# A two-layer hybrid decoder step on one core: page table in one transfer, sums of squares by token, and the prompt's products moved from GpSimd to VectorE

## Chip, cores and metric

The kernel runs on one core of a Trainium2 chip. The metric is the device time of one execution in microseconds (us); three unprofiled runs of the kernel before gave 2775.24, 2779.84 and 2781.72 us, median 2779.84 us.

## The reference, cut to what matters

Two layers of a decoder trunk work on a prompt (16 meta tokens and 512 tokens) and on a sample group (8 sequences of 8 new tokens with 2048 cached positions each), 592 token columns in all. Every layer does

```
x += 0.5 * SwiGLU_1(rmsnorm(x))
h  = rmsnorm(x);  [z|xBC|dt|q|k|v] = h @ w_in
SSD group: causal conv, chunked state-space scan, gate, grouped rmsnorm
SB group:  q, k normed per head, stick-breaking attention, rmsnorm
x += concat(ssd, sb) @ w_out
x += 0.5 * SwiGLU_2(rmsnorm(x))

rms_norm(x)  = x / sqrt(mean(x*x) + 1e-6) * gain
sb attention: z = q.k/8 + bias;  log_stay = log_sigmoid(-z) (0 where masked)
              w = exp(log_sigmoid(z) + sum of log_stay over later keys);  o = w @ v
cached keys and values: cache[l][page_table], page_table is 8 x 16 int32
```

So each norm needs, for each token, the sum of squares over the model dimension; stick-breaking weights are a sigmoid times a running product of "stays" from the right; and the cached keys and values are found through the page table.

## The kernel before, in words

**Layout.** Activations lie feature-major: a tile holds 128 features (partitions) by 592 tokens (columns), eight tiles make the model dimension. A weight matrix is multiplied in units of 128 output features (`gemm`, L618). `raw` (L570) loads 512 KB of float32 weights into one of three buffers by a DMA that SyncE (SP) issues; `split` (L576) makes a rounded high part `whi` on ScalarE (L581) and a remainder `wlo` on VectorE (L582); `mm3` (L585) then issues three products for each of 8 feature tiles and each of two column halves of 296 tokens (L590): 48 products a unit, into two PSUM banks. After every product `step` (L595) advances the generators in `self.flows`, so small work is written in between the large products, one piece a product.

**Norms.** The large products run on values that are not yet divided by the norm; the factor R is applied when a unit is drained (`times_r`, L226). `factor` (L539) makes R in a flow, six times through `norm_end` (L565, two tiles of squares, `acc` and `sq`, L443 to L453) and twice in `mix_sb` (L1247, four tiles of squares). The flow is: some waiting steps; `sums` (L459): float32 products with a block of ones as the stationary operand and 512 and then 80 (or 64) columns of squares moving, for each tile of squares its own strip of output rows; `by_token` (L466): two ScalarE copies out of PSUM and five PE transposes, so that tokens lie on partitions; `gather_sums` (L484): small VectorE copies and additions; `rsqrt` (L504): some 14 VectorE instructions of 128x5; 20 waiting steps; `spread` (L518): ten products that spread the result over 128 rows; two ScalarE copies into R (L559). While the flow runs, `self.hold` keeps units from being drained. `queries` (L784) does the same for eight heads a token with four tiles of squares, one flow a tile, and then makes the scaled queries `qs` on which the sample's attention starts. `head_norm` (L851) and `normed` (L1195) use the same helpers.

**Page table.** `setup_rest` (L275), written in the program after the first of the three parts of the first feed-forward block, loads constants. L331 to L335 load the page table in 20 DMAs, already spread as the gathers want it: 16 into `ptk` (8 partitions by 8 entries each) and 4 into `ptv` (32 partitions by 32 entries), both constant tiles with a buffer of their own. L338 to L353 make the row numbers `ki` and `vi` of them on VectorE; the gathers of keys (L1462) and values (L1526) on GpSimd (POOL) read those. Other loads of `setup_rest` (L286, L294) go into the shared temporary buffers (`tmp`, tag "t", six of them).

**Prompt attention.** `pair_blocks` (L1288) runs 12 times a layer and does two heads each time: PE products z, two sigmoids on ScalarE (L1314, L1315), the running product `stay` on VectorE (L1273), and then the product of the two on POOL (L1318); in `rest` PE transposes it (L1325) and multiplies with the values. The same stretch has the sample's attention over the cached pages (`past`, L1433): gathers on POOL, 32x32 transposes on VectorE (L1468), and so on.

**Order.** The program is written once in a straight line; the framework's scheduler then orders each engine's instructions by a model of their times and by priorities, and an engine runs its queue strictly in that order. Within `mixer`, `ahead` (L605) gives work earlier priorities from the tables `PRI` and `UNIT` (L94 to L102), due times counted in instructions from the point `p0` (L711). Instructions whose operands are ready early in the model can be moved far ahead of where they are written, if their tile has a free buffer.

Of the kernel before, what the change touches and what calls it, by code (L numbers as in the profile page):

```python
# [11 lines left out]
I32 = mybir.dt.int32  # L12
AF = mybir.ActivationFunctionType
ALU = mybir.AluOpType
# [13 lines left out]
def const_arrays():  # L28
    p = np.arange(128)
    f = np.float32  # L30
    a32 = np.arange(32)
    c = {}
    c["ident"] = np.eye(128)
    c["ones"] = np.ones((128, 1))
    c["half"] = p[:, None] // 64 == np.arange(32)[None, :]
    o8 = np.zeros((128, 64))
    q64 = np.arange(64)
    same = q64[:, None] // 8 == q64[None, :] // 8
    o8[:64] = same
    c["one8"] = o8  # L40
    c["srep"] = p[:, None] % 32 == p[None, :] % 32
    a16 = np.arange(16)[None, :]
    c["sel16"] = (p[:, None] % 8 == a16 % 8) & (p[:, None] // 32 % 2 == a16 // 8)
    c["mko"] = ((p[:, None] // 8) % 4 == np.arange(4)[None, :])
    sm = np.zeros((128, 8))
    sm[:64] = q64[:, None] // 8 == np.arange(8)[None, :]
    c["seqm"] = sm
    dsel = np.zeros((128, 8))
    for h in range(8):
        dsel[h, h] = 1.0  # L50
        dsel[32 + h, h] = 1.0
    c["dsel"] = dsel
    c["koff"] = ((p % 8) * 16)[:, None]
    c["voff"] = ((p % 32) * 4)[:, None]
    c["kt16"] = np.broadcast_to(np.arange(16)[None, :], (128, 16))
    return {k: np.ascontiguousarray(v.reshape(128, -1)).astype(f) for k, v in c.items()}

# [47 lines left out]
class Kern:  # L105
# [169 lines left out]
    def setup_rest(self):  # L275
# [49 lines left out]
            nc.vector.tensor_copy(o[:, 0], v)  # L325
            nc.vector.tensor_scalar(o[:, 1], v, -1.0, None, ALU.mult)

        ptk = self.cst([128, 8], "ptk", I32)
        ptv = self.cst([128, 32], "ptv", I32)
        pt = I["page_table"]  # L330
        for g in range(16):  # L331
            nc.sync.dma_start(ptk[8 * g:8 * g + 8, :], pt[:, g].partition_broadcast(8))
        ptr = pt.rearrange("b (a x) -> x (b a)", x=4)
        for x in range(4):
            nc.sync.dma_start(ptv[32 * x:32 * x + 32, :], ptr[x].partition_broadcast(32))  # L335
        kf = self.cst([128, 8], "kf")
        vf = self.cst([128, 32], "vf")
        nc.vector.tensor_copy(kf, ptk)  # L338
        nc.vector.tensor_copy(vf, ptv)
        nc.vector.tensor_scalar(kf, kf, 128.0, self.c_koff, ALU.mult, ALU.add)  # L340
        nc.vector.tensor_scalar(vf, vf, 128.0, self.c_voff, ALU.mult, ALU.add)
        nc.vector.tensor_scalar(kf, kf, 0.5, None, ALU.mult)
# [116 lines left out]
    def sums(self, A, B, x, w, t, sel):  # L459

        n = self.c1 - self.c0 - 512
        for p, c, m in ((A, self.c0, 512), (B, self.c0 + 512, n)):
            self.nc.tensor.matmul(p[w * x:w * x + w, 0:m], sel, t[:, c:c + m], start=True, stop=True)  # L463
            yield

    def by_token(self, A, B, wait):  # L466

        nc = self.nc
        n = self.c1 - self.c0
        s = self.tmp("sums")  # L470
        nc.scalar.activation(s[:, 0:512], A, AF.Copy)
        nc.scalar.activation(s[:, 512:n], B[:, 0:n - 512], AF.Copy)
        for _ in range(wait):
            yield
        for i in range(4):
            nc.tensor.transpose(A[:, 128 * i:128 * i + 128], s[:, 128 * i:128 * i + 128], self.ident)
            yield
        nc.tensor.transpose(B, s[:, n - 128:n], self.ident)
        yield
# [4 lines left out]
    def gather_sums(self, A, B, n, w):  # L484

        nc = self.nc
        v = self.tok("rv", n=n)
        pA, pB = A.rearrange("p (g c) -> p g c", c=128), B.unsqueeze(1)
        for p, o in ((pA, v[:, 0:4]), (pB, v[:, 4:5])):
            if w:  # L490
# [13 lines left out]
    def rsqrt(self, v, n, inv):  # L504

        nc = self.nc
        y, w, hi, lo = self.tok("ry", n=n), self.tok("rw", n=n), self.tok("rhi", F32R, n), self.tok("rlo", F32R, n)
        nc.vector.tensor_scalar(v, v, inv, 1e-6, ALU.mult, ALU.add)
        nc.vector.tensor_scalar(y.bitcast(I32), v.bitcast(I32), -0.5, float(0x5f3759df), ALU.mult, ALU.add)
        for _ in range(3):  # L510
            nc.vector.tensor_tensor(w, y, y, ALU.mult)
# [27 lines left out]
    def factor(self, squares, inv, wait):  # L539
# [5 lines left out]
        def flow():  # L545
            for _ in range(wait[0]):
                yield
            A, B = self.own("po", [128, 512]), self.own("pw", [128, 128])
            w = 128 // len(squares)
            for x, s in enumerate(squares):  # L550
                yield from self.sums(A, B, x, w, s, self.c_ones.to_broadcast([128, w]))
            yield from self.by_token(A, B, wait[1])
            y, r = self.rsqrt(self.gather_sums(A, B, 1, w), 1, inv)
            nc.vector.tensor_copy(rt, y)
            for _ in range(wait[2]):
                yield
            yield from self.spread_all(r, 0, 1, A, B)
            for p, o in self.both(A, B, R):
                nc.scalar.activation(o, p, AF.Copy)  # L559
            self.hold = False  # L560
# [223 lines left out]
    def queries(self, win):  # L784
# [8 lines left out]
        def flow(m, s):  # L793
            for _ in range(wait[0]):
                yield
            yield from self.sums(A, B, m, 32, s, self.c_half)
            if m < 3:
                return
            yield from self.by_token(A, B[:, 0:128], wait[1])
            v = self.gather_sums(A, B[:, 0:128], 8, 0)  # L800
            rt2 = self.tok("rt2", n=1)
            nc.vector.tensor_tensor(rt2, self.rt, self.rt, ALU.mult)
            nc.vector.tensor_tensor(v, v, rt2.to_broadcast([128, 5, 8]), ALU.mult)
            y, r = self.rsqrt(v, 8, 1.0 / 64)
            self.r8, self.nr8 = (self.small(n, [128, 5, 8], bufs=1) for n in ("r8", "nr8"))
            for _ in range(wait[2]):
# [481 lines left out]
    def pair_blocks(self, q, k, OT, m, blocks, i):  # L1288
# [3 lines left out]
        o = 0  # L1292
# [14 lines left out]
        for hp in range(2):  # L1307
# [7 lines left out]
                nc.scalar.activation(s[:, s0:s0 + n], zv, AF.Sigmoid, scale=self.nr8[:, b, h:h + 1], bias=self.nb[:, c:c + 1])  # L1315
                self.stay(s, 128, s0, s0 + n)

            nc.gpsimd.tensor_tensor(e[:, 0:o - 1], e[:, 0:o - 1], s[:, 1:o], ALU.mult)  # L1318

        def rest():  # L1320
            wt = []
# [275 lines left out]
```

## Time and profile before

| | us |
|---|---|
| median of three runs | 2779.84 |
| the profiled execution | 2797.72 |
| its span (first to last instruction) | 2795.9 |
| PE (matmul) busy in it | 2656.9 |
| VectorE (DVE) busy | 1502.2 |
| ScalarE (ACT) busy | 994.7 |
| GpSimd (POOL) busy | 356.9 |
| mean granted PE clock, share of 2.4 GHz | 0.973 |

The profiled execution took 17.9 us longer than the median of the unprofiled runs. In the rows below, PE is the matmul array and PEld its weight loads; a matmul's duration holds its time through the pipeline, so products that follow each other 0.13 us apart are shown with 0.30 us each. A row of idle time names what ended the wait ("<-").

### The profile page before, as it was taken

The page shows a single profiled execution, that of the slowest core. Times are in us where ns is not written, and L with a number is a line of the kernel's source. Part 1 is how long each engine was busy: PE and PEld are TensorE (multiplying, and loading weights), DVE is VectorE, ACT ScalarE, POOL GpSimd, SP SyncE. Part 2 cuts the span into 40 slices and gives each one's busy share as a digit, 9 for nine tenths or more (in the row PEclk, how much of TensorE's full clock was granted, in tenths as well). Part 3 has the DMA queues.
Part 4 walks back from the last instruction along what each step waited for, and adds up shares of the span by engine and source line. Part 5 has one row for each costly group of instructions (what it writes and reads, how often), then busy time and mean ns, then how long its engine had stood idle before and what let it go on. Part 6 is the DMA issues. An engine that isn't in the chain of part 4 may idle for free.

```text
span 2795.9 us, 51271 instructions
## 1 busy us (share of the span) xinstructions
PE 2656.9 (95%) x21469; PEld 2472.6 (88%) x21469; DVE 1502.2 (54%) x2978; ACT 994.7 (36%) x1795; POOL 356.9 (13%) x336
## 2 busy tenths in 40 slices
PE   6999999999877999999999999999997789999999
PEld 5999999887655899999999999998885568999999
DVE  4444445386768564343554343454776776444444
ACT  2222224255645332222332222233565543322222
POOL 1000000023356010000000000000334541000000
PEclk8999999999979999999999999999998899999999
DMA  3232234347677222222222322244576772222222
GB/s 100 76 93 93 79 106 134 113 145 258 204 233 241 100 69 85 82 76 88 72 84 76 105 77 92 87 145 126 169 248 203 250 236 69 78 89 80 88 77 87
DMA packets 250279, 343.22 MB, mean 123 GB/s; under 512 B 38104, under 2 KB 201888, under 8 KB 250048
## 3 DMA queue, kind: packets, MB, share of 16 engines
q1 hardware_dynamic: 213184, 205.71, 23.8%
q0 software_dynamic: 36864, 134.23, 14.4%
q8 instruction: 168, 2.75, 0.4%
q14 instruction: 63, 0.52, 0.1%
HBM read 320.23 MB, written 19.66 MB: 122 GB/s over the span
## 4 chain that ended last, share of the span: by engine, by line
PE 59%; DVE 3%; ACT 2%; DMA 1%; issue 1%; POOL 0%; another core or an unknown queue 0%; SPq 0%; DVEq 0%; ACTq 0%; POOLq 0%
PE g L590 52%; PE v L905 1%; DMA v<-in_cache_v,vi 1%; DVE kt L1468 1%; PE po L206 1%; PE po L463 0%; PE po L209 0%; PE sc L209 0%; DMA kn<-in_cache_k,ki 0%; PE z L209 0%; POOL v L1526 0%; PE z L206 0%; ACT L1090 0%; ACT dec L1090 0%; DVE x L777 0%
## 5 line engine op out<-in xcount | busy, mean ns | idle before, releaser
L590 PE MATMUL g<-xh,wlo 128*128 128x296 f32 (+1 forms) x3392 | 1014.6, 300 | 17.3 <-DVE wlo L582 17.3
L590 PE MATMUL g<-xl,whi 128*128 128x296 f32 (+1 forms) x3392 | 1015.9, 300 | 2.7 <-DVE xl L441 2.7
L590 PE MATMUL g<-xh,whi 128*128 128x296 f32 (+1 forms) x3392 | 1014.7, 300 | 2.4 <-DVE gs L229 2.0
L581 ACT ACTIVATE whi<-raw 128x512 fp32r<-128x512 f32 (+1 forms) x664 | 413.9, 624 | 1342.5 <-PE g L590 1271.1
L582 DVE TENSOR_TENSOR wlo<-raw,whi 128x512 fp32r<-128x512 f32 (+1 forms) x664 | 450.9, 679 | 614.5 <-ACT whi L581 568.4
L590 PEld LDWEIGHTS g<-xh,wlo 128*128 128x128 f32 x3392 | 640.4, 189 | 20.6 <-DVE wlo L582 17.9
L590 PEld LDWEIGHTS g<-xh,whi 128*128 128x128 f32 x3392 | 640.0, 189 | 10.5 <-issue 6.3
L590 PEld LDWEIGHTS g<-xl,whi 128*128 128x128 f32 x3392 | 640.5, 189 | 7.5 <-DVE xl L441 3.6
L590 PE MATMUL g<-hl,whi 128*128 128x296 f32 (+1 forms) x1408 | 417.9, 297 | 0.0
L590 PE MATMUL g<-hh,wlo 128*128 128x296 f32 (+1 forms) x1408 | 417.7, 298 | 0.0
L590 PE MATMUL g<-hh,whi 128*128 128x296 f32 (+1 forms) x1408 | 416.8, 298 | 0.0
L1462 POOL DMA_INDIRECT kn<-in_cache_k,ki x128 | 134.7, 1052 | 1590.6 <-PE g L590 1104.8
L590 PEld LDWEIGHTS g<-hl,whi 128*128 128x128 f32 x1408 | 265.2, 188 | 0.0
L590 PEld LDWEIGHTS g<-hh,wlo 128*128 128x128 f32 x1408 | 264.3, 188 | 0.0
L590 PEld LDWEIGHTS g<-hh,whi 128*128 128x128 f32 x1408 | 263.9, 188 | 0.0
L1468 DVE STREAM_TRANSPOSE kt<-kn 128x512 f32<-128x512 f32 x256 | 162.9, 681 | 29.0 <-PE pS L1097 7.5
L1526 POOL DMA_INDIRECT v<-in_cache_v,vi x128 | 139.1, 1087 | 252.3 <-DVE kt L1468 121.3
L686 DVE SCALAR_TENSOR_TENSOR x<-g,x 128x296 f32<-128x296 f32 (+1 forms) x192 | 88.2, 464 | 120.5 <-PE g L590 119.9
L229 DVE TENSOR_TENSOR us<-g,R 128x296 f32<-128x296 f32 (+1 forms) x176 | 81.5, 464 | 128.0 <-PE g L590 127.9
L229 DVE TENSOR_TENSOR gs<-g,R 128x296 f32<-128x296 f32 (+1 forms) x176 | 80.7, 464 | 125.9 <-PE g L590 120.0
L673 ACT ACTIVATE hh<-us 128x592 fp32r<-128x592 f32 (+1 forms) x88 | 61.4, 698 | 63.3 <-DVE us L671 63.3
L209 PE MATMUL sc<-kt,qbd 128*32 128x128 f32 x1920 | 79.0, 291 | 3.7 <-issue 3.6
(387 smaller groups left out, 2993.2 us busy)
## 6 DMA issues: line engine op xcount, KB each, us to landing
raw<-in_ffn_w_gu SPq DMA_DIRECT2D x176, 512.0 KB
raw<-in_ffn_w_down SPq DMA_DIRECT2D x80, 512.0 KB
raw<-in_w_in SPq DMA_DIRECT2D x44, 512.0 KB
raw<-in_w_out SPq DMA_DIRECT2D x16, 512.0 KB
spill<-x SPq DMA_DIRECT2D x16, 296.0 KB
x<-spill SPq DMA_DIRECT2D x16, 296.0 KB
raw<-in_ffn_w_down SPq DMA_DIRECT2D x16, 256.0 KB
xt<-in_x_prompt SPq DMA_DIRECT2D x8, 256.0 KB
```

What stands on the lines that cost most here:

```text
L206: i = self.nc.tensor.matmul(*a, **k).ins
L209: i = self.nc.tensor.matmul(*a, **k).ins
L229: self.nc.vector.tensor_tensor(tv[0:P, h, :], ps[h][0:P, 0:self.n], rv[0:P, h, :], ALU.mult)
L581: nc.scalar.activation(hi[:, 0:nk], s, AF.Copy)
L582: nc.vector.tensor_tensor(lo[:, 0:nk], s, hi[:, 0:nk].bitcast(F32), ALU.subtract)
L590: nc.tensor.matmul(ps[h][:, 0:self.n], w[:, k, :], self.hv(x)[:, h, :], start=(first and k == 0 and i == 0), stop=(last and k == nk - 1 an ...
L673: nc.scalar.activation(hh[:, a:b], u[:, a:b], AF.Copy)
L686: nc.vector.scalar_tensor_tensor(v, p, 0.5, v, ALU.mult, ALU.add)
L905: nc.tensor.matmul(ps[c], x[:, t0:t0 + 128], w.rearrange("p x c -> p (x c)"), start=(k == 0 and i == 0), stop=(k == 7 and i == 2))
L1462: nc.gpsimd.indirect_dma_start(kn, None, self.kflat, bass.IndirectOffsetOnAxis(ap=self.kidx[l][:, s, i:i + 1], axis=0))
L1468: nc.vector.transpose(kt[:, 2 * u:2 * u + 2].rearrange("p t h i -> p t (h i)"), kns[u][:, :, 256 * quad:256 * quad + 256])
L1526: nc.gpsimd.indirect_dma_start(v.rearrange("p k c -> p (k c)"), None, self.vflat, bass.IndirectOffsetOnAxis(ap=self.vidx[l][:, i, e:e + 1] ...
```

## The change

Five things are changed and nothing else. (1) The page table is loaded by one DMA into all 128 partitions (a temporary tile), made float32, and the entries that a partition needs are picked by a product with a 0/1 mask (two new constants, `mg` and `mx`) and halving additions on VectorE. (2) `factor` uses the new `token_sums`: for each group of 128 tokens and each tile of squares one float32 product with the squares as the stationary operand and one column of ones moving, so that the sums come out with tokens on partitions; the copies, transposes and gathering additions of that norm are gone. (3) `queries` does the same with two columns for its two heads a tile. (4) Two helpers get tiles of their own (`rg`, `rv`, `rq`). (5) The product of L1318 goes from GpSimd to VectorE.

```diff
@@ const_arrays
+    c["mg"] = p[:, None] // 8 == a16
+    c["mx"] = p[:, None] // 32 == np.arange(4)[None, :]
@@ setup_rest
-        ptk = self.cst([128, 8], "ptk", I32)
-        ptv = self.cst([128, 32], "ptv", I32)
-        pt = I["page_table"]
-        for g in range(16):
-            nc.sync.dma_start(ptk[8 * g:8 * g + 8, :], pt[:, g].partition_broadcast(8))
-        ptr = pt.rearrange("b (a x) -> x (b a)", x=4)
-        for x in range(4):
-            nc.sync.dma_start(ptv[32 * x:32 * x + 32, :], ptr[x].partition_broadcast(32))
+        pti = self.tmp("pti", [128, 128], I32)
+        nc.sync.dma_start(pti, I["page_table"].rearrange("b g -> (b g)").partition_broadcast(128))
+        ptf, sel = self.tmp("ptf", [128, 128]), self.tmp("sel", [128, 128])
+        nc.vector.tensor_copy(ptf, pti)
         kf = self.cst([128, 8], "kf")
         vf = self.cst([128, 32], "vf")
-        nc.vector.tensor_copy(kf, ptk)
-        nc.vector.tensor_copy(vf, ptv)
+        for out, m in ((kf, self.c_mg), (vf, self.c_mx)):
+            n, k = out.shape[1], m.shape[1]
+            sv = sel.rearrange("p (a g) -> p a g", g=k)
+            nc.vector.tensor_tensor(sv, ptf.rearrange("p (a g) -> p a g", g=k),
+                                    m.unsqueeze(1).to_broadcast([128, n, k]), ALU.mult)
+            while k > 1:
+                k //= 2
+                d = out.unsqueeze(2) if k == 1 else sv[:, :, 0:k]
+                nc.vector.tensor_tensor(d, sv[:, :, 0:k], sv[:, :, k:2 * k], ALU.add)
@@ Kern
+    def token_sums(self, out, squares, sel):
+        for i, t0 in enumerate(self.groups()):
+            for x, t in enumerate(squares):
+                self.nc.tensor.matmul(out[:, i], t[:, t0:t0 + 128], sel, start=(x == 0), stop=(x == len(squares) - 1))
+                yield
@@ gather_sums
-        v = self.tok("rv", n=n)
+        v = self.tok("rg", n=n)
@@ rsqrt
-        nc.vector.tensor_scalar(v, v, inv, 1e-6, ALU.mult, ALU.add)
+        s, v = v, self.tok("rv", n=n)
+        nc.vector.tensor_scalar(v, s, inv, 1e-6, ALU.mult, ALU.add)
@@ factor
-            w = 128 // len(squares)
-            for x, s in enumerate(squares):
-                yield from self.sums(A, B, x, w, s, self.c_ones.to_broadcast([128, w]))
-            yield from self.by_token(A, B, wait[1])
-            y, r = self.rsqrt(self.gather_sums(A, B, 1, w), 1, inv)
+            P = B[:, 0:5].unsqueeze(2)
+            yield from self.token_sums(P, squares, self.c_ones)
+            y, r = self.rsqrt(P, 1, inv)
@@ queries
-            yield from self.sums(A, B, m, 32, s, self.c_half)
+            P = A[:, 0:40].rearrange("p (g h) -> p g h", g=5)
+            yield from self.token_sums(P[:, :, 2 * m:2 * m + 2], [s], self.c_half[:, 0:2])
             if m < 3:
                 return
-            yield from self.by_token(A, B[:, 0:128], wait[1])
-            v = self.gather_sums(A, B[:, 0:128], 8, 0)
-            rt2 = self.tok("rt2", n=1)
+            rt2, v = self.tok("rt2", n=1), self.tok("rq")
...
-            nc.vector.tensor_tensor(v, v, rt2.to_broadcast([128, 5, 8]), ALU.mult)
+            nc.vector.tensor_tensor(v, P, rt2.to_broadcast([128, 5, 8]), ALU.mult)
@@ pair_blocks
-            nc.gpsimd.tensor_tensor(e[:, 0:o - 1], e[:, 0:o - 1], s[:, 1:o], ALU.mult)
+            nc.vector.tensor_tensor(e[:, 0:o - 1], e[:, 0:o - 1], s[:, 1:o], ALU.mult)
```

## Rows read from the trace of the kernel before

**Rows 1.** The page: span, and busy time of each engine.
```profile
span 2795.9 us, 51271 instructions
PE 2656.9 (95%) x21469; PEld 2472.6 (88%) x21469; DVE 1502.2 (54%) x2978; ACT 994.7 (36%) x1795; POOL 356.9 (13%) x336
```

**Rows 2.** Windows: stretch and length, busy us of each engine, PEclk, DMA share, GB/s.
```profile
0.00:100.00 100.00, 72.51 (x442) 66.17 (x443) 47.32 (x109) 29.87 (x54) 13.54 (x21) 0.88 0.34 91
...
740.00:900.00 160.00, 121.23 (x1355) 81.82 (x1352) 117.94 (x241) 83.77 (x176) 89.36 (x84) 0.83 0.68 221
...
2120.00:2260.00 140.00, 111.43 (x1207) 76.31 (x1206) 107.25 (x217) 80.42 (x166) 77.23 (x72) 0.83 0.67 218
```

**Rows 3.** Windows of L590 alone: length, PE and PEld busy (count), PEclk, DMA.
```profile
100.00:120.00 20.00, 20.00 (x150) 20.00 (x149) 1.00 0.26 80
40.00:72.00 32.00, 9.77 (x42) 9.24 (x43) 0.63 0.23 52
...
481.70:494.80 13.10, 10.58 (x72) 9.61 (x70) 1.00 0.45 141
```

**Rows 4.** Timeline of VectorE, ScalarE, PE in the start-up: start, length, operation [idle before].
```profile
55.51 0.18 DVE L339 CAST vf<-ptv 128x32 f32<-128x32 int32 x1 [20.50 <-DMA ptv<-in_page_table]
...
55.88 0.68 DVE L582 TENSOR_TENSOR wlo<-raw,whi 128x512 fp32r<-128x512 f32 x1
...
55.79 0.35 ACT L989 ACTIVATE dtw<-dtr 128x32 fp32r<-128x32 f32 x2 [19.61 <-DMA dtr<-in_w_in]
...
56.62 0.61 PE L590 MATMUL g<-xh,wlo 128*128 128x296 f32 x1 [16.64 <-DVE wlo L582]
```

**Rows 5.** Timeline of SyncE's DMA queue in the start-up: start, time to issue.
```profile
15.19 5.48 SPq L332 DMA_DIRECT2D ptk<-in_page_table  x9
...
24.95 2.48 SPq L332 DMA_DIRECT2D ptk<-in_page_table  x7
...
32.50 12.40 SPq L335 DMA_DIRECT2D ptv<-in_page_table  x4
44.94 3.19 SPq L984 DMA_DIRECT2D dtr<-in_w_in  x1
```

**Rows 6.** Line 286: shortest/median/longest issue in ns, first and last start.
```profile
L286 SPq DMA_DIRECT2D mt<-in_c_mask x2: 374/412/450, 156.9 to 157.4; - x2
```

**Rows 7.** Groups of VectorE by form: busy, mean ns; the nearest to the new operations.
```profile
L242 DVE CAST identr<-call 128x128 fp32r<-128x128 f32 x1 | 0.2, 227 | 1.9 <-DMA call<-in_c_const 1.9
...
L964 DVE TENSOR_TENSOR xc<-cacc,u 128x528 f32<-128x528 f32 x12 | 8.5, 711 | 2.9 <-ACT u L962 1.9 <-issue 1.0
```

**Rows 8.** Timeline of PE: sums of a norm between large products; four small products (L1543).
```profile
483.04 1.07 PE L463 MATMUL po<-sq,call 128*64 128x512 f32 x2
484.04 0.41 PE L590 MATMUL g<-xh,whi 128*128 128x296 f32 x1
...
650.96 0.62 PE L1543 MATMUL po<-call,ob 128*128 128x16 f32 x4
```

**Rows 9.** Timeline of PE in the second layer's output norm.
```profile
2328.69 1.07 PE L463 MATMUL po<-gsq,call 128*32 128x512 f32 x6
...
2340.01 0.33 PE L206 MATMUL po<-identr,rhi 128*128 128x128 f32 x1 [2.21 <-DVE rhi L514]
```

**Rows 10.** Groups of POOL by form: busy, mean ns, idle before.
```profile
L1318 POOL TENSOR_TENSOR be<-be,st 128x511 f32<-128x511 f32 x32 | 35.7, 1117 | 20.4 <-DVE st L1273 17.3 <-DVE te L1064 1.9 <-issue 0.8
...
L1318 POOL TENSOR_TENSOR be<-be,st 128x255 f32<-128x255 f32 x16 | 15.0, 947 | 18.7 <-DVE st L1273 15.4 <-DVE rv L498 3.1
```

**Rows 11.** Line 1505 on VectorE: ns shortest/median/longest; its group: busy, mean.
```profile
L1505 DVE SCALAR_TENSOR_TENSOR pbe<-pbe,cq,pst x32: 711/741/2202, 616.6 to 2295.0; 128x511 f32<-128x511 f32 x32
...
L1505 DVE SCALAR_TENSOR_TENSOR pbe<-pbe,cq,pst 128x511 f32<-128x511 f32 x32 | 28.7, 898 | 0.2
```

**Rows 12.** Waits of PE: us in total, times, longest.
```profile
PE po L206 <- DMA v<-in_cache_v,vi: 16.3, 9, 7.5
...
PE zt L1325 <- POOL be L1318: 6.0, 5, 3.1
```

## The prediction, made before the change was run

> **What bounds the kernel now.** I read the page first: PE is busy 2656.9 of 2795.9 us [rows 1], so at most 139 us of the span are PE's idle time, and what shortens the kernel is either such idle time or PE work. The windows then show where it is idle: 27.5 us in the first 100 us, 38.8 us in the first layer's mixing stretch (740 to 900) and 28.6 us in the second's (2120 to 2260), where the granted clock is 0.83 too [rows 2]. In the feed-forward blocks PE has no gap: 150 large products in 20 us, one every 0.133 us [rows 3].
>
> The timeline of the start-up shows the one large wait of the program. VectorE stood 20.50 us at the cast of `ptv`; the `wlo` behind it in its queue came only then, and PE waited 16.64 us for that [rows 4]. On SyncE's queue the 20 page-table DMAs took 5.48, 2.48 and 12.40 us to issue, 20.4 us in all [rows 5]. ScalarE stood beside it, 19.61 us for `dtr` [rows 4], which SyncE could issue only after them [rows 5].
>
> **The change part by part.**
>
> *The page table.* Twenty DMAs go, one of 128 rows of 512 bytes comes. Its target is now a temporary tile of tag "t". The other constants that load into that tag were not pulled ahead into the start-up: `mt` was issued at 156.9 us [rows 6], when the first feed-forward part no longer wants these buffers. I expect the new transfer and all that hangs on it (`ptf`, `kf`, `vf`, `ki`, `vi`, and on POOL's queue the first gathers of keys) there too; the sample's scores need them only in the mixer, after the whole block. The new VectorE work is one cast, two products and six additions of at most 128 columns: 9 by 0.23, the nearest row, a cast of 128x128 [rows 7], 2.1 us, between feed-forward products where PE's own time covers it; if it were at the start-up instead, 2 us is what it costs.
>
> What goes: between 40 and 72 us PE did 42 large products [rows 3], which at 0.133 are 5.6 us; with ten spreading products and five transposes at 0.12 (below), 1.8 us, that is 7.4 us of work in 32. So 24.6 us were lost, of them 16.64 the wait itself. The rest, 8.0 us, is half clock (0.63 mean in that window [rows 3]) and the wait for R. Without the gap the clock should hold, and R's chain of small VectorE instructions runs beside the next unit; but three units of 48 products fill the six PSUM banks, so a part of the wait for R stays. I take 16.6 and two thirds of 8.0: **-22**. Bounds: -24.6 if all goes, -10 if another late load takes over (first rival).
>
> *Sums by token, PE's work.* A norm of two tiles now: in the 13.1 us from 481.7 PE did 72 large products, 9.6 us, so sums and transposes cost 3.5 us. After: ten products, each two passes (as the eight instructions of today's four sums show). Four small ones with a 128-column stationary operand took 0.62 us, about 0.12 from start to start [rows 8]: 20 by 0.12 is 2.4. Each time a float32 product stands between the large ones there is more: the large product behind one shows 0.41 instead of 0.30 [rows 3, 8]; I take 0.2 an excursion for both edges, and five excursions (the half on `acc` is ready early, that on `sq` goes in one run): 3.4. So -0.1 a norm, six norms, -0.6. The output norm loses: today its sums run side by side in strips, six passes in 1.07 us [rows 9], in all about 3.3 with the transposes; after, 40 by 0.12 is 4.8: +1.5, twice, +3. Queries: four tiles at about 1.4 each [rows 8] and 0.6 of transposes, 6.2; after, 40 by 0.12 and four excursions, 5.6: twice -0.6. Sum about **+1**.
>
> *Sums by token, the wait for R.* Two ScalarE copies, the transposes and six small VectorE instructions leave the chain to R. Where PE had run out of banks this shows: the second layer's output norm waited 2.21 us for `rhi` [rows 9], and the waits at the start-up are counted above. I take -2.2 there and about -1 for the other places: **-3**. In the flow the steps of a norm go from 47 to 48, so that in a unit of 48 products the release of `hold` slips behind the unit's end and its drain is written one unit later; the scheduler orders by readiness and three units fit the banks, so I cost it at nothing. If it binds it is some 1 us at each of six norms. Norms together **-2**, bounds -6 and +8.
>
> A rule of the Trainium skill says otherwise of PE's work. The row first: two passes of 512 columns took 1.07 us, 0.5 apart [rows 8]. The page "TensorE: Matmul & The Clock Gate", section "Back-to-back issue gap", prices a product at its columns over 2.4 GHz plus 2.5 ns (0.216 us for 512), and its section "LDWEIGHTS (loading the stationary operand)" a load at columns over 1.2 GHz (0.107 us for 128). By it today's norm would be 4 by 0.216, 4 by 0.036 and 5 by 0.107, 1.5 us, and the new one 20 by 0.107, 2.1 us: the change would lose 0.6 a norm, six times, and the total would be 4 us less of a gain. The trace's 3.5 us does not agree with it, so I keep the rows.
>
> *The products on VectorE.* POOL spent 35.7 and 15.0 us on 32 and 16 of them [rows 10]. On VectorE a product of 528 columns of float32 took 0.711 [rows 7], so 0.69 for 511 and at most 0.41 for 255: 22 + 6.6 = 28.6 us over both layers. Against it: L1505 has a median of 0.741 but a longest of 2.202 us [rows 11], and its slow ones fall on times when POOL runs such a product; its mean is 0.898, so 32 by 0.157, 5 us, come back, and the scans suffer in the same way. Net about +23 in stretches where VectorE is busy 118 of 160 and 107 of 140 us [rows 2], so three quarters of the time; I put a quarter of it on the path: +6. Queued behind each new instruction are the transposes and splits of the same stretch. On the other side POOL no longer stands waiting for scans (17.3 + 15.4 us [rows 10]) ahead of its gathers, and PE waited 6.0 us for these products and 16.3 for gathered values [rows 12]: I take all of the first and a fifth of the second, -9. Sum **-3**. Bounds: -15 with both waits gone and no cost, +23 with all of it on the path.
>
> **The sum**: -22 - 2 - 3 = -27 us, against the profiled execution's 2797.7 (span 2795.9 and 1.8 around it): 2770.7. The runs shown have a median 17.9 us lower; I take the same 27 us off it: 2779.8 - 27 = **2753**.
>
> **Rivals.**
> 1. *Another late load takes the stall's place.* ScalarE waited for `dtr` nearly as long as VectorE for the table [rows 4]. It landed within 10.9 us of its issue at 44.94 [rows 4, 5]. Issued at 32.5 and as slow, it would hold ScalarE to 43 us, and PE would still stop for some 4; or the new table is pulled ahead and VectorE waits for it. Against: `dtr` was slow because 4-byte transfers were ahead of it. The start-up then gives -12, the whole -17: **2763**.
> 2. *VectorE becomes the bound of the mixing stretches (slower).* It decides once VectorE is busy more than about 95% there: 118 + 14 of 160 is 83%, which speaks against; that VectorE's queue is strictly in order speaks for, since a late scan then holds the transposes behind it. Then the whole 28.6 is on the path, and with a clock of 0.83 [rows 2] that falls further in longer PE gaps I add half: +43, with -25 from the rest +18: slower, **2797**.
> 3. *The new order gives back what the start-up gains.* Priorities inside the mixer are counted in instructions and the scheduler models times; other times there mean another order of the whole stretch, in which PE idles 67 us today [rows 2]. A loss of 40% of that, 27, is no change: **2780**.
>
> **How the numbers follow.** Forecast 0.70, rival 1 0.14, rival 2 0.08, rival 3 0.08. About 0.2%, 5.6 us, is what a measurement of this kernel can tell from no change. Faster: 0.70 + 0.14 and a quarter of rival 3's spread, 0.86; same 0.05 and slower 0.09 from the rest of it and rival 2. The likeliest case by its own bounds (the start-up 2 better to 5 worse, norms 4 better to 5 worse, products 10 better to 8 worse, not all at once) is 2740 to 2765. The range reaches past rival 1 above and a little below: 2735 to 2773.
>
> **What would show it.** Right: no wait of VectorE for a page-table transfer; PE's idle time in the first 100 us below 13 us instead of 27.5; the 42 products after the 40th us done by about 50; no L1318 on POOL, 48 more products on VectorE at 0.6 to 0.7 us, L1505 without values near 2 us; no wait for `rhi` in the second output norm; PE's extra at a norm still about 3.4. Wrong: a gap of over 5 us at the start-up behind ScalarE's `dtw` or the new cast; VectorE over 95% busy between 740 and 900; PE idle there above 50 us.

## The result and the profile after

The changed kernel took 2739.24 us (median of four runs, 2729.76 to 2747.8) against 2779.51 of the kernel before beside it: ratio 0.986, 95% interval 0.9833 to 0.9887, 40.3 us less. The forecast was 2753 (27 less), range 2735 to 2773. The profiled execution took 2746.03 us, its span is 51.9 shorter than the one of [rows 1]; 11 of that is the spread between executions, since before's profiled execution lay 17.9 above its median and this one 6.8.

The page of the changed kernel, and its windows at the times of [rows 2] (what stands in a window is some 20 us further on in the program than before):

```profile
span 2744.0 us, 51377 instructions
PE 2641.0 (96%) x21587; PEld 2497.2 (91%) x21587; DVE 1502.8 (55%) x2993; ACT 976.7 (36%) x1769; POOL 313.4 (11%) x288
```
```profile
0.00:100.00 100.00, 90.18 (x595) 85.72 (x596) 53.53 (x109) 34.92 (x61) 12.44 (x20) 0.97 0.34 102
740.00:900.00 160.00, 138.00 (x1521) 106.15 (x1519) 115.07 (x256) 76.61 (x165) 59.70 (x56) 0.89 0.67 229
2120.00:2260.00 140.00, 118.43 (x1328) 89.55 (x1328) 99.93 (x230) 67.00 (x145) 53.17 (x48) 0.91 0.67 227
```

PE is idle 9.8 us in the first 100 instead of 27.5, and 22.0 instead of 38.8 from 740 to 900; the granted clock is higher in all three. VectorE, which got 48 products more, is not busier over the span (1502.8 us against 1502.2).

To see where the 51.9 us come from I took marks on PE's timeline, each the start of a named large product, and subtracted:

| from, to | before | after | difference |
|---|---|---|---|
| start to the first product of the first down projection (`g<-hh`) | 154.3 | 134.3 | -20.0 |
| end of a first feed-forward block to the last value product, both layers | 63.3, 63.4 | 60.5, 60.5 | -5.7 |
| mixing stretch: last value product to the last product of the first half of `w_out` (`g<-mh`), both layers | 441.4, 435.8 | 426.4, 423.7 | -27.1 |
| all else | 1637.6 | 1638.6 | about +1 |

The two stretches as windows (columns as in [rows 2]), before, then the changed kernel:

```profile
544.90:986.30 441.40, 387.82 (x3945) 313.39 (x3944) 311.06 (x684) 220.30 (x451) 159.53 (x147) 0.93 0.60 196
1924.80:2360.60 435.80, 385.61 (x3945) 312.08 (x3944) 310.91 (x685) 222.92 (x453) 161.02 (x148) 0.93 0.60 199
```
```profile
522.20:948.60 426.40, 382.41 (x3963) 320.32 (x3962) 311.52 (x700) 215.45 (x444) 136.93 (x123) 0.92 0.60 203
1884.40:2308.10 423.70, 382.74 (x3964) 318.62 (x3963) 308.98 (x700) 214.07 (x442) 137.48 (x123) 0.93 0.60 204
```

PE's idle time in them falls from 53.6 and 50.2 us to 44.0 and 41.0, at nearly the same granted clock. The two mixing stretches carry half of the 51.9, and in the prediction's sum they have only -3. That is what the experiments are about.

**The start-up** is as forecast. L602 (before: L590) in the windows of [rows 3], then the longest gap between large products that is left there, and the page table with what used to wait for it (SyncE, VectorE):

```profile
40.00:50.00 10.00, 7.88 (x46) 7.49 (x45) 0.84 0.17 54
...
40.00:72.00 32.00, 29.88 (x202) 29.49 (x201) 0.93 0.16 52
```
```profile
15.14 0.38 SPq L995 DMA_DIRECT2D dtr<-in_w_in  x1
...
31.51 0.37 SPq L995 DMA_DIRECT2D dtr<-in_w_in  x1
...
47.80 0.41 PE L602 MATMUL g<-xh,whi 128*128 128x296 f32 x1 [1.22 <-DVE gs L231]
...
139.55 0.51 SPq L332 DMA_DIRECT2D pti<-in_page_table  x1
...
143.80 0.23 DVE L334 CAST ptf<-pti 128x128 f32<-128x128 int32 x1 [1.14 <-DMA pti<-in_page_table]
```

In the 32 us where PE had done 42 large products it now does 202. The wait of 16.64 us [rows 4] is gone, and no gap between large products in the first 100 us is longer than the 1.22 us behind `gs`. The new transfer goes out at 139.55, late, as `mt` did [rows 6], and VectorE waits 1.14 us for it under feed-forward products. The two transfers of `dtr`, of which the first left SyncE at 44.94 [rows 5] and the second at 57.77, leave at 15.14 and 31.51.

**The products and their neighbours**, groups of VectorE by form (line, form, count, busy and mean, idle before):

```profile
L1329 DVE TENSOR_TENSOR be<-be,st 128x511 f32<-128x511 f32 x32 | 21.1, 664 | 0.0
...
L1516 DVE SCALAR_TENSOR_TENSOR pbe<-pbe,cq,pst 128x511 f32<-128x511 f32 x32 | 23.7, 739 | 0.2
...
L1284 DVE TENSOR_TENSOR_SCAN st<-st,zero 128x255 f32<-128x255 f32 x16 | 10.7, 675 | 2.6 <-ACT st L1326 2.6
...
L1329 DVE TENSOR_TENSOR be<-be,st 128x255 f32<-128x255 f32 x16 | 6.4, 408 | 0.1
```
```profile
L1273 DVE TENSOR_TENSOR_SCAN st<-st,zero 128x255 f32<-128x255 f32 x16 | 14.3, 899 | 5.4 <-ACT st L1315 5.4
```

The last line is the kernel before's. The products cost 21.1 + 6.4 = 27.5 us. L1516 (L1505 in [rows 11]) fell from 28.7 to 23.7, the scan of 255 columns from 14.3 to 10.7: with no GpSimd product beside them these two groups give back 8.6 of the 27.5 us.

### The profile page after: what moved, and what is told of

It is laid out like the page before. It is cut to its first block, busy times and chain, and to the rows that moved or that the text cites. A ratio compares the mean times of both kernels' runs of the same rounds, so it can differ in the third digit from the quotient of the medians.

```text
span 2744.0 us, 51377 instructions
## 1 busy us (share of the span) xinstructions
PE 2641.0 (96%) x21587; PEld 2497.2 (91%) x21587; DVE 1502.8 (55%) x2993; ACT 976.7 (36%) x1769; POOL 313.4 (11%) x288
## 3 DMA queue, kind: packets, MB, share of 16 engines
q1 hardware_dynamic: 208016, 205.77, 23.7%
## 5 line engine op out<-in xcount | busy, mean ns | idle before, releaser
L602 PE MATMUL g<-xl,whi 128*128 128x296 f32 (+1 forms) x3392 | 1018.7, 301 | 0.9 <-DVE xl L447 0.9
L602 PE MATMUL g<-xh,wlo 128*128 128x296 f32 (+1 forms) x3392 | 1013.5, 300 | 3.4 <-DVE wlo L594 3.4
L602 PE MATMUL g<-xh,whi 128*128 128x296 f32 (+1 forms) x3392 | 1014.9, 300 | 1.6 <-DVE gs L231 1.2
L602 PEld LDWEIGHTS g<-xh,wlo 128*128 128x128 f32 x3392 | 641.4, 189 | 5.8 <-DVE wlo L594 4.1
L602 PEld LDWEIGHTS g<-xh,whi 128*128 128x128 f32 x3392 | 640.4, 189 | 6.6 <-issue 3.0
L602 PEld LDWEIGHTS g<-xl,whi 128*128 128x128 f32 x3392 | 641.7, 189 | 4.0 <-issue 2.2
L602 PE MATMUL g<-hl,whi 128*128 128x296 f32 (+1 forms) x1408 | 417.8, 297 | 0.0
L602 PE MATMUL g<-hh,wlo 128*128 128x296 f32 (+1 forms) x1408 | 417.7, 298 | 0.0
L602 PE MATMUL g<-hh,whi 128*128 128x296 f32 (+1 forms) x1408 | 416.7, 298 | 0.0
L1473 POOL DMA_INDIRECT kn<-in_cache_k,ki x128 | 142.5, 1113 | 1546.7 <-PE g L602 931.4
L602 PEld LDWEIGHTS g<-hl,whi 128*128 128x128 f32 x1408 | 265.2, 188 | 0.0
L602 PEld LDWEIGHTS g<-hh,wlo 128*128 128x128 f32 x1408 | 264.4, 188 | 0.0
L602 PEld LDWEIGHTS g<-hh,whi 128*128 128x128 f32 x1408 | 263.9, 188 | 0.0
L602 PE MATMUL g<-mh,whi 128*128 128x296 f32 (+1 forms) x256 | 83.0, 332 | 4.8 <-ACT mh L1267 4.6
L602 PE MATMUL g<-ml,whi 128*128 128x296 f32 (+1 forms) x256 | 85.1, 333 | 0.0
```

The lines of the kernel that those rows point to most:

```text
L602: nc.tensor.matmul(ps[h][:, 0:self.n], w[:, k, :], self.hv(x)[:, h, :], start=(first and k == 0 and i == 0), stop=(last and k == nk - 1 an ...
L1473: nc.gpsimd.indirect_dma_start(kn, None, self.kflat, bass.IndirectOffsetOnAxis(ap=self.kidx[l][:, s, i:i + 1], axis=0))
```

## The experiments

Eleven kernels were timed against the kernel before, and the kernel before was profiled once more. They ran in three groups, each group on one chip; the kernel before had medians of 2799.52, 2774.78 and 2805.62 us there, so differences and ratios are taken within a group. "Stretch 1" and "stretch 2" are the mixing stretches of the table above, in the profiled execution of each kernel; they vary by several us from one execution to the next and with the chip, so only large differences are read from them.

Of these three chips the kernel before was profiled on the third group's only (before_again). What its two stretches take together on each chip can be estimated: its median there, less the 1918.7 us that its first profile has outside the stretches (2795.9 - 877.2) and the 1.8 around the span, leaves 879 us in the first group, 854 in the second and 885 in the third. The last column is a kernel's two stretches less that, after taking off by how much its profiled execution lay above its median: an estimate. table_only and before_again, whose stretches have the old order, come out at +2 and -1 where 0 would be right. The same sum for the changed kernel's first profile gives -16, not the -27 of the table above.

| kernel | median, before's | ratio, 95% interval | start-up | stretch 1, 2 | both, against before's (estimate) |
|---|---|---|---|---|---|
| table_only | 2784.05, 2799.52 | 0.9936 (0.9917 to 0.9955) | 136.3 | 445.9, 442.4 | +2 |
| sums_only | 2766.69, 2799.52 | 0.9871 (0.9851 to 0.9892) | 148.7 | 423.4, 436.7 | -19 |
| products_only | 2805.92, 2799.52 | 1.0023 (1.0009 to 1.0037) | 154.9 | 452.8, 428.8 | +5 |
| no_products | 2757.46, 2799.52 | 0.9844 (0.9824 to 0.9864) | 132.5 | 418.4, 447.1 | -14 |
| due_584 | 2786.40, 2774.78 | 1.0037 (1.0024 to 1.0051) | 155.2 | 452.1, 413.4 | +8 |
| queries_only | 2750.52, 2774.78 | 0.9914 (0.9899 to 0.9928) | 154.5 | 421.3, 417.6 | -26 |
| factor_only | 2773.95, 2774.78 | 0.9989 (0.9978 to 1.0001) | 147.7 | 424.3, 439.8 | +9 |
| after_again | 2728.91, 2774.78 | 0.9843 (0.9822 to 0.9863) | 131.1 | 424.4, 420.0 | -18 |
| queries_584 | 2836.86, 2805.62 | 1.0109 (1.0090 to 1.0129) | 154.4 | 460.7, 456.5 | +32 |
| after_584 | 2782.43, 2805.62 | 0.9920 (0.9903 to 0.9937) | 130.7 | 448.3, 449.6 | +7 |
| before_again | one run, 2810.39 | - | 155.1 | 445.4, 443.1 | -1 |
| no_products_due | 2766.38, 2805.62 | 0.9850 (0.9832 to 0.9869) | 132.6 | 441.3, 441.7 | -13 |

**First group: one part at a time.** Three theories of the mixing stretches' gain. A: it is the products', whose place on GpSimd had held up gathers and scans. B: it is the sums', because the sample's scaled queries come 5.8 us earlier and the output norm is shorter. C: it is neither; every edit makes the scheduler plan another order, and the order that came out is a shorter one.

*table_only*: the kernel before with this alone.

```diff
-        for g in range(16):
-            nc.sync.dma_start(ptk[8 * g:8 * g + 8, :], pt[:, g].partition_broadcast(8))
...
+        nc.sync.dma_start(pti, I["page_table"].rearrange("b g -> (b g)").partition_broadcast(128))
```

> Only the page table's part of the change on the kernel before. Theory A (each part works in its own place): the 20 us at the start-up are this part's, and nothing else moves: 20 us less than the kernel before (16 to 23), the mixing stretches within 4 us of it. Theory B (the gain behind the start-up is the sums' by token): the same here. Theory C (whatever is edited, the planner writes another order of the mixing stretches, and that order is what gained there): the mixing stretches move here too, by 8 us or more a layer, up or down, so the sum lies outside 16 to 23.

Measured: 15.5 us less, just under the 16 to 23 of A and B. In the profile the start-up is 18.0 shorter, and PE's order in both stretches is the old one, group by group; so the 4.5 and 6.6 us by which these stretches are longer here than in the kernel before's first profile are the spread between executions and chips. The price of the page table's part is the start-up's 18.

*sums_only*: the kernel before with `token_sums` in `factor` and in `queries`, and the tiles `rg`, `rv`, `rq`.

```diff
-                yield from self.sums(A, B, x, w, s, self.c_ones.to_broadcast([128, w]))
...
+            yield from self.token_sums(P, squares, self.c_ones)
...
-            yield from self.sums(A, B, m, 32, s, self.c_half)
...
+            yield from self.token_sums(P[:, :, 2 * m:2 * m + 2], [s], self.c_half[:, 0:2])
```

> Only the sums by token, in factor and in queries, with the tiles of their own, on the kernel before; table and products as before. Theory A: 2.8 us less in front of each mixer and about 1 at each output norm: 5 to 9 us less than the kernel before; the stretch from the last value product to the last product of w_out within 4 us of before in each layer. Theory B: those stretches' gain (15 and 12 us) is of this part, since the scaled queries are there earlier and the output norm is shorter: 25 to 33 us less. Theory C: those stretches move by 8 us or more, in a direction that no part explains.

Measured: 32.8 less, as B says. But B wants both stretches shorter. Against table_only, which has the old order on the same chip (445.9, 442.4), the first is 22.5 us shorter and the second 5.7, which is within the spread. PE's list of instructions in stretch 1 agrees with the old one to 0.76 (equal neighbours taken as one; twice the matching runs over the length of both lists, 1 for equal lists), in stretch 2 to 0.98. The stretch that was planned anew became short, the other one hardly.

*products_only* and *no_products*: the product on VectorE in the kernel before, and back on GpSimd in the changed one.

```diff
-            nc.gpsimd.tensor_tensor(e[:, 0:o - 1], e[:, 0:o - 1], s[:, 1:o], ALU.mult)
+            nc.vector.tensor_tensor(e[:, 0:o - 1], e[:, 0:o - 1], s[:, 1:o], ALU.mult)
```

> Only the prompt's products moved to VectorE, on the kernel before. Theory A: the mixing stretches' gain is of this part: GpSimd has no product in front of its gathers and VectorE's scans run without GpSimd beside them: 20 to 28 us less than the kernel before, 10 to 15 in each layer's stretch from the last value product to the last product of w_out, PE's idle time in 740 to 900 us under 30 us. Theory B (and the prediction's own term): 3 us less. Theory C: any value between 15 less and 15 more, unequal in the two layers.

> The changed kernel with the prompt's products back on GpSimd: table and sums by token stay. Theory A: 20 to 28 us more than the changed kernel, that is 12 to 20 us less than the kernel before, all of it in the mixing stretches; PE's granted clock in the window that holds the prompt's pairs back to about 0.83. Theory B: within 5 us of the changed kernel. Theory C: the mixing stretches move by 8 us or more, but products_only and this one don't add up to the same size.

Measured: with the products alone the kernel is 6.4 us slower; without them the rest is 42.1 less. A has fallen: that part does not gain (the 6.4 hold a new order too, with stretches of 452.8 and 428.8). Other VectorE work did get faster, as the page of products_only shows:

```profile
PE 2668.0 (95%) x21469; PEld 2478.6 (88%) x21469; DVE 1506.5 (54%) x3026; ACT 987.1 (35%) x1791; POOL 307.9 (11%) x288
```

48 products of 27.7 us together came to VectorE and its busy time rose by 4.3 us against [rows 1]; POOL lost 49.0. The kernel's time did not fall by it.

**Second group: order against part.** Now B' (the queries' earlier start shortens the stretches) against C' (the order alone does). due_584 changes one due time of the scheduler's table `UNIT` in the kernel before, the first one of the sample's scores, and no instruction:

```diff
-    "prompt6": 106, "prompt7": 1403, "ps0": 507, "ps3": 2030, "ps4": 1648, "ps7": 1031, "pv0": 0, "pv3": 1421,
+    "prompt6": 106, "prompt7": 1403, "ps0": 584, "ps3": 2030, "ps4": 1648, "ps7": 1031, "pv0": 0, "pv3": 1421,
```

> The kernel before with one number of its table of due times changed (ps0 507 to 584): no instruction is added, removed or moved to another engine, only the scheduler's order of the mixing stretches becomes another. In the second layer PE's order is then 0.91 like that of sums_only's first layer and only 0.65 like the old second layer's; in the first layer it is like none seen. Theory C' (a mixing stretch costs what its order makes it cost, 436 to 447 us from the last value product to the last product of w_out in the old second-layer order, 418 to 429 in the orders of the changed kernel, whatever the parts): second stretch 418 to 430, first one anywhere from 415 to 455; the sum 30 less to 10 more. Theory B' (the stretch became shorter because the scaled queries are there 5.8 us earlier): second stretch unchanged, 434 to 447.

Measured: 11.6 us more, just outside what C' allowed (30 less to 10 more); stretches of 452.1 and 413.4, the second below the 418 to 430 of C'. One number that adds no work made one stretch the shortest of all kernels and the other longer than in any kernel of the first group but one, and the total slower: together the two are some 8 us longer than before's on this chip, by the estimate, which is most of the 11.6. The change has no instruction in it, so here the order alone is the cause.

*queries_only* has only the second half of sums_only's diff (with the tiles), *factor_only* only the first.

> Only the sums by token of queries, with the tiles of their own, on the kernel before. PE's order in the first mixing stretch is 0.98 like sums_only's, in the second 0.81 like the old one's. Theory C': first stretch 418 to 429 us, second 434 to 447 (before 441 and 436), little elsewhere: 12 to 25 us less than the kernel before. Theory B': both stretches shorter by the same 10 or more.

> Only the sums by token of factor, with the tiles of their own, on the kernel before. PE's order is 0.98 (first stretch) and 0.91 (second) like the old one's. Theory C': stretches of 439 to 447 and 434 to 447 us as before, the gain only from the shorter chain to R: about 5.6 at the start-up and 1 or 2 elsewhere, 4 to 9 us less than the kernel before. Theory B' says the same here; what would speak against both is a gain above 12 us, from output norms or from the norms in the feed-forward blocks.

Measured: 24.3 less and 0.8 less. queries_only has both stretches short (421.3, 417.6), which fits B' better than C' in the second, where C' had put 434 to 447 by a likeness of 0.81 to the old order. factor_only keeps the start-up's gain of 6.6 us but shows almost none of it in its median, so its stretches should have given it back: at 424.3 and 439.8 they are shorter than in the first profile of the kernel before, but some 9 us longer than before's by the estimate for this chip. The 424.3 is also below what C' said. So the lengths alone did not decide between B' and C'. The timeline does. The first score products behind the last value product on PE, and the first sigmoids on them on ScalarE, in the kernel before (stretch begins at 544.90):

```profile
547.57 0.30 PE L206 MATMUL sc<-kt,qbd 128*32 128x128 f32 x1
...
578.16 0.48 ACT L1267 ACTIVATE pbe<-sc,bq 128x256 f32<-128x256 f32 x1
578.54 0.47 ACT L1268 ACTIVATE pst<-sc,bq 128x256 f32<-128x256 f32 x1
```

and in the changed kernel (522.20):

```profile
524.80 0.30 PE L208 MATMUL sc<-kt,qbd 128*32 128x128 f32 x1
...
555.39 0.47 ACT L1278 ACTIVATE pbe<-sc,bq 128x256 f32<-128x256 f32 x1
555.76 0.47 ACT L1279 ACTIVATE pst<-sc,bq 128x256 f32<-128x256 f32 x1
```

The scaled queries (`qs`) are written from 6.0 us ahead of the last value product before and 11.8 after, and `qbd`, the copy of them that the scores read, is complete 1.9 us ahead of the first score product before and 7.7 after; yet the first score product starts 2.6 to 2.7 us behind it in both, because PE's queue has it there, and the first sigmoid 33.2 to 33.3 behind it in both. The 5.8 us end there, in stretch 1, where this was read. PE's order is the same in both kernels for the first 75 us of stretch 1 and 77 of stretch 2; only then do they part.

*after_again* is the changed kernel, unedited, beside these.

> The changed kernel itself, beside the others on one chip. Parts measured on one chip: table 15.5 less, sums 32.8 less, products 6.4 more, sum 41.9 less; table and sums together 42.1 less. Theory A (the products gain where gathers no longer stand behind them): 50 us or more less than the kernel before. Theory C' (at like orders the products on VectorE cost 5 to 9 us a stretch, and the second layer's new order gives back about 20): 40 to 55 less. No gain or loss from the products at all: 42 less.

Measured: 45.9 less. The parts measured alone add up to 41.9 (15.5 + 32.8 - 6.4), no_products to 42.1: the products change nothing that can be told.

**Third group: the same part in another order.** queries_584 is queries_only, after_584 the changed kernel, each with the one number of due_584.

> queries_only with the one number of due_584 (ps0 507 to 584): the sums by token of queries stay, only the scheduler's order of the mixing stretches becomes another. PE's order is now 0.97 like due_584's in the first stretch and 0.91 like the old one's in the second. Theory C' (the order sets a stretch's length, the part itself gains only about 1.5 us in front of each mixer): as long as due_584's first stretch and before's second one, 445 to 455 and 434 to 447 us on a chip like the first; 2 to 15 us more than the kernel before. Theory B' (the sums by token of queries shorten the mixing stretches themselves): the gain of queries_only stays, 15 to 25 us less than the kernel before, or at least 20 less than due_584 stood (+10), that is 10 less than before.

> The changed kernel, all parts, with that one number of the table of due times changed. PE's order in the first mixing stretch is then 0.81 like due_584's (the long one) and 0.61 like the changed kernel's, in the second 0.80 like the old one's. Theory C': the gain up to the first mixer stays (22 to 26 us), the 15 to 25 of the mixing stretches go: 5 to 28 us less than the kernel before. Theories that put the gain on a part (A, B, B'): 38 to 50 less, as the changed kernel.

> The kernel before itself, for a profile on the same chip as the others of this call: start-up and feed-forward blocks within 1 us of its first profile; the two mixing stretches (441 and 436 us there) may differ by the granted clock, 5 to 15 us, at the same idle time of PE (within 4 us of 54 and 50).

Measured: queries_584 is 31.2 us slower than the kernel before, where queries_only was 24.3 faster; same instructions, 55 us apart by one due time, each against the kernel before on its own chip. after_584 is 23.2 less instead of 45.9 or 40.3: the start-up's gain is all there (130.7) and the stretches' is gone. The kernels with 507 and with 584 ran on different chips, so part of these two differences may be the chips'; for the order speak that 584 is the slower number in all three pairs, due_584's on one chip among them, and that no_products_due, below, has its gain on the third group's chip. B' has fallen, and so has every theory that gives the stretches' gain to a part whatever the order. The windows of the two stretches (columns as in [rows 2]), queries_only, then queries_584, then before_again:

```profile
543.70:965.00 421.30, 383.20 (x3944) 311.54 (x3943) 308.15 (x684) 216.54 (x447) 159.13 (x147) 0.94 0.62 206
1903.10:2320.70 417.60, 375.18 (x3945) 305.95 (x3944) 312.16 (x681) 217.61 (x446) 162.15 (x147) 0.94 0.62 207
```
```profile
543.50:1004.20 460.70, 399.63 (x3944) 323.22 (x3943) 316.02 (x685) 225.09 (x454) 156.78 (x148) 0.89 0.57 188
1942.60:2399.10 456.50, 400.71 (x3944) 318.98 (x3943) 313.04 (x683) 221.98 (x448) 161.68 (x148) 0.89 0.58 190
```
```profile
545.70:991.10 445.40, 394.56 (x3944) 316.94 (x3944) 311.51 (x684) 220.17 (x452) 160.35 (x147) 0.92 0.60 195
1929.70:2372.80 443.10, 395.94 (x3945) 318.41 (x3944) 311.60 (x684) 222.86 (x452) 161.88 (x148) 0.90 0.60 195
```

before_again came out as expected: the start-up within 1 us, PE's idle time within 4, the stretches 4.0 and 7.3 longer at a lower clock. There are 3944 or 3945 matmuls in each line, and VectorE, ScalarE and POOL are busy alike within 4%. What differs is PE's idle time (38.1 and 42.4 us, 61.1 and 55.8, 50.8 and 47.2) and its granted clock. C' had said 2 to 15 more for queries_584, and its second stretch 434 to 447; it came out at 456.5, though PE's order there is 0.91 like the old one. So that the order moves the length is shown; how long an order is can't be read from its likeness to another, a tenth that differs is enough.

*no_products_due* looked for something better than the changed kernel: products on GpSimd, and one other due time.

```diff
-    "scan3": 879, "scan5": 123, "wo0": 0, "wo1": 2358, "wo2": 1775, "wo3": 86, "wo4": 1087, "wo5": 1599, "wo6": 529,
+    "scan3": 1046, "scan5": 123, "wo0": 0, "wo1": 2358, "wo2": 1775, "wo3": 86, "wo4": 1087, "wo5": 1599, "wo6": 529,
```

> The changed kernel with the products back on GpSimd and one other number of the table of due times changed (scan3 879 to 1046): PE's order in the first stretch is 0.80 like the changed kernel's, in the second 0.81. Theory C': both stretches of the short kind, so 40 to 55 us less than the kernel before, as good as the changed kernel or some 5 better, with the products on either engine. Theory A (the products on VectorE gain): 12 to 30 less.

Measured: 39.2 less, just under the 40 to 55 of C' and above the 12 to 30 of A; ratio 0.985, the changed kernel's within the intervals. Its profiled execution was 10.8 above its median, and the stretches in it, 441.3 and 441.7, are not the lengths that C' gave; against before's on this chip they are some 13 us shorter by the estimate. No version beat the changed kernel.

## Why the prediction was right, and where it was not

**Page table, -22: right.** Its signs are there: no long wait of VectorE, 9.8 us idle in the first 100 (below 13), 46 products done between 40 and 50, `dtr` early, the new transfer at 139.55. Measured alone the part gives 18.0 at the start-up, the shorter chain to R another 5.6 (sums_only) or 6.6 (factor_only), and together 20.0 to 24.4 in five profiles with both (against 154.3, or 155.1 in the third group): so most of the two thirds of the 8.0 us beside the wait belongs to the sums, not to the table.

**Norms, PE's work, +1: the excursions were wrong, in count and price.** A norm in the changed kernel, L602 in a window with one norm, and the sums on PE's timeline:

```profile
461.70:474.40 12.70, 10.94 (x79) 10.54 (x78) 1.00 0.46 146
```
```profile
466.60 2.06 PE L476 MATMUL pw<-call,sq 128*128 128x1 f32 x18
```

18 of the 20 passes ran in one go, 0.11 us apart (the 0.12 of [rows 8] held), and the two of one product stood alone: two excursions, not the five that I had costed. The norm costs 12.7 - 79 x 0.133 = 2.2 us instead of 3.5, so -1.3 and not -0.1, and the sign "about 3.4" did not come. 20 passes at 0.11 are those 2.2 already, so the 0.2 for the edges of an excursion does not show either. In front of each mixer, one norm and the queries, 2.8 us went. At the other norms little shows: the marks there move by -0.9 to +1.1, in sum about +1; what takes it back was not tried. The Trainium skill's page "TensorE: Matmul & The Clock Gate", section "LDWEIGHTS (loading the stationary operand)", prices a load at its columns over 1.2 GHz; 20 loads of 128 columns are 2.1 us by that estimate. The trace's 2.2 agrees with it. It was the old norm where the page's sum, 1.5 us, and the trace, 3.5, parted, and the trace was the one to keep.

**Wait for R, -3.** No wait of PE for `rhi` is left in the second output norm, as said. Norms together gave -5.7 in front of the mixers and about +1 elsewhere, against -2, inside the bounds of -6 and +8 (their 5.6 at the start-up stand under the page table, as in the prediction).

**Products, -3: no gain.** The durations were right (0.664 and 0.408 us for 0.69 and 0.41, no L1516 above 0.751). VectorE's net was put at +23 and is 27.5 less what the neighbours give back, +4.3 in products_only. What failed is the other side, "all of the first and a fifth of the second". PE's wait for these products fell, from 6.0 to 2.2 us, but the one for gathered values [rows 12] rose from 16.3 to 30.7:

```profile
PE po L208 <- DMA v<-in_cache_v,vi: 30.7, 21, 4.6
...
PE zt L1336 <- DVE be L1329: 2.2, 2, 1.2
```

It rose in the kernel whose stretches are shorter, and in before_again, which is the old kernel, it is 11.6 instead of 16.3. Its size was no measure of what could be gained.

**The sum, -27.** What the parts do outside the mixing stretches is about -25 in the profiles (20.0 and 5.7, less the 1 elsewhere). The -24 for the start-up and the norms was thus right; of the products' -3 nothing was seen. after_584's -23.2 is no proof of the sum, since its own order made its stretches some 7 us longer by the estimate. The median's other 15 us or so come from the mixing stretches, and the runs with one due time changed put them down to the new order. That is rival 3's mechanism ("the new order gives back what the start-up gains"), which I had priced as a loss of up to 27 and at 0.08; it came out as a gain of that kind, and as a loss in due_584 and queries_584. That the result lies in the range is luck in part: its lower end lay 18 below the forecast, but no gain from a new order was in it.

**Rivals 1 and 2 did not come.** No late load took the stall's place, and VectorE is busy 115.07 of 160 us.

**Open** is what in an order makes a stretch long. The idle times and the clock were seen, their cause in the queue was not found.

## What to carry to other kernels

Where a scheduler writes the queues, an edit has two effects: its own work, which the rows of the profile price well, and a new order of a crowded stretch, which they don't price at all. Measure the second before you credit a part: change one neutral number of the planning and time the kernel again; here that moved the total by 12 us on one chip, and by 55 between two chips, the latter more than all parts together. A sum for such a change wants this spread, on both sides, in its range.

## What the runs showed of the hardware that was not expected

PE's busy time for nearly the same products differs by a tenth, and with it the granted clock. Stretch 2 of due_584, then of no_products:

```profile
1937.70:2351.10 413.40, 372.04 (x3944) 305.89 (x3943) 309.24 (x682) 215.29 (x448) 156.15 (x147) 0.95 0.62 209
```
```profile
1872.50:2319.60 447.10, 405.69 (x3963) 331.30 (x3962) 308.39 (x675) 220.26 (x446) 159.85 (x147) 0.88 0.58 194
```

PE is idle 41.4 us in both; the 33.7 us between them are busy time, at a mean granted clock of 0.95 and 0.88 of full speed (it is granted 1.2 or 2.4 GHz). These two are from different chips and orders, and the second has 19 products more. The order is not needed for such a difference: stretch 2 of the kernel before took 385.61 us busy at 0.93 in its first profile and 395.94 at 0.90 in before_again, with PE's order the same (0.999). How much the order adds, no run here separates.

Work of GpSimd is paid for on VectorE too: taking 49.0 us of products off POOL and putting 27.7 onto VectorE raised VectorE's busy time by only 4.3 us (products_only; L1505 and the scans gave back 11.8 of it, the rest is spread over other work). Of the 32 L1505 in the kernel before, the four that overlapped a product on POOL took 1.73 to 2.20 us and the other 28 at most 0.752; in products_only the longest took 0.789, in the changed kernel 0.751.
